# Up projection by seven Strassen block products on normed operands, down projection as its own stage

## The chip, the cores and the metric

The kernel runs on one core of a Trainium2 chip. A core has five engines with queues of their own: TensorE (PE, matrix products into PSUM; its weight loads are listed as PEld), VectorE (DVE), ScalarE (ACT), GpSimd (POOL) and SyncE (SP, which here only issues DMAs). The metric is the device time of one execution in microseconds (us), lower is better.

## The reference

One layer of a streaming encoder, for 1024 tokens of width 1024: a mixer (latent attention and a gated linear recurrence side by side, then an output projection with a residual), a feed-forward block, and a gated embedding. What matters here is the end:

```python
hf = rms_norm(x, g_ffn)
up = causal_dwconv(hf @ w_up, w_ffn_conv, b_ffn_conv)     # 1024 -> 2 * 2816, then 3 taps along the tokens
gte, val = up[..., :2816], up[..., 2816:]
x = x + (gelu(gte) * val) @ w_down                        # 2816 -> 1024
gate = sigmoid(rms_norm(x, g_ple) @ w_ple_gate + b_ple_gate)
x = x + gate * (p @ w_ple)
```

Everything is float32 at the interface. `rms_norm` divides by the root mean square over the 1024 channels and multiplies by a gain.

## The kernel before

Activations lie transposed: channels on the 128 partitions, tokens along the free axis. The residual x is eight channel tiles `x1[k][h]`, each in two halves h of 512 tokens. Every product is made of three matmuls, since each operand is split into a rounded high part and a rest, both in the fp32r type: high by high, high by low, low by high (`three`, L133). A split (`split`, L111) is an ACT cast for the high part and a DVE subtraction for the low part. With a gain, it is `scaled` (L116). `wload` (L121) brings a 128x1024 weight tile by DMA and splits it, in two-buffer tags `whi` and `wlo`. A matmul here has 128 rows, 128 output channels and 512 tokens, and is counted as one.

**Mix (L748 to L795).** For each half h, eight output channels c, each with two chains of 12 matmuls (`lru` and `at`), and four DVE operations on PSUM and x1 (L774, L775, L791, L792). After the loop of a half, `gained` (L837) makes from every x1 tile the split operand `h[k][h]` (ACT L118, DVE L119) and adds its square to a running sum (ACT L831, and L835 on DVE, or on POOL where `pool=True`). `measure` (L845, `stats` L139) sums the squares over partitions with eight small matmuls (L145) and takes the power -1/2 on POOL (L150). `scale` (L849, `spread` L153) spreads the result over partitions with two matmuls (L165), and ACT copies it to `r1` (L851).

**Feed-forward (L855 to L919).** 22 units j, each with a gate and a value block z of 128 channels. For each block PE runs 2 x 24 matmuls on the raw, gained operands, and the norm comes after the product: DVE multiplies the PSUM result by `r1` (L894). ACT makes the first tap with the bias (L896), DVE the other two (L898), ACT the gelu (L901), DVE the product of the two blocks (L902), which is split (L905). The down projection runs between the units, two units at a time (`GROUP`): 8 channels x 2 halves x 2 units x 3 matmuls, each PSUM result added to x1 by DVE (L873). The last two groups are done half by half, with `gained` for the gate's norm after each half (L914 to L918).

**Gate (`ple`, L940 to L969).** 16 chains of 24 matmuls, both halves of a channel in turn; the half's `measure` and `scale` come after the second and third chain for h = 0, after the fifth and sixth for h = 1. Four steps for each result: times r1 (L965), sigmoid (L966), times the embedding (L967), plus x1 (L968), and out by DMA. The embedding `e` was made during attention (`embed`, L921) and put in DRAM.

The order of each engine's instructions is the framework's: the order of the code is a priority, and an instruction whose inputs are late lets later ones go ahead. So the small matmuls of the gate's first `measure` stand in the trace at 1190.32 us, ahead of the gate's chains, which the code has first.

Of the kernel before, what the change touches and what calls it, by code (L numbers as in the profile page):

```python
# [19 lines left out]
P = 128  # L20
# [10 lines left out]
NL = 4  # L31
FF = 2816
NF = FF // P
GROUP = 2
# [41 lines left out]
class Block:  # L76
# [30 lines left out]
    def chain(self, out, terms, start=True, stop=True):  # L107
        for n, (w, x) in enumerate(terms):
            self.nc.tensor.matmul(out, lhsT=w, rhs=x, start=start and n == 0, stop=stop and n == len(terms) - 1)  # L109
# [104 lines left out]
    def project(self):  # L214
# [125 lines left out]
        self.ew.tile([P, 512], F32, name="pad1")  # L340
# [407 lines left out]
    def mix(self):  # L748
# [4 lines left out]
        self.r1 = x1p.tile([P, S], F32, name="r1")  # L753
        mx, ws, V = self.mx, self.wo, nc.vector
        self.mix_lru(1)
        self.h = [[None] * 2 for _ in range(NK)]
# [4 lines left out]
        for h in range(2):  # L761
# [8 lines left out]
            for c in range(NK + 2):  # L770
# [14 lines left out]
                if h == 1 and c == 4:  # L785
                    self.measure("x1", 0, D)
                if h == 1 and c == 5:
                    self.scale("x1", 0)
                if c >= 2:
                    o = at[c - 2]  # L790
                    V.tensor_tensor(out=o, in0=o, in1=self.r1[:, hs], op=ALU.mult)  # L791
                    V.tensor_tensor(out=self.x1[c - 2][h], in0=o, in1=self.x1[c - 2][h], op=ALU.add)  # L792
            self.gained(h, "g_ffn", "x1")
# [43 lines left out]
    def gained(self, h, gain, key, pool=False):  # L837

        nc = self.nc
        for k in range(NK):  # L840
            self.h[k][h] = self.pair(h)
            self.scaled(self.x1[k][h], self.col(gain, k), *self.h[k][h])
            self.square((key, h), k, self.x1[k][h], pool)
# [10 lines left out]

    def ffn(self):  # L855
        nc = self.nc
        V = nc.vector
        self.banks(sm=3, big=2)
        cf, fp = self.pool("ffn", 1, side="right")
        G, Wd = [], []  # L860

        def down(h, G, Wd, last=False):
            hs = slice(h * HALF, (h + 1) * HALF)
            for c in range(NK):
                if last and c % 3 == 1:
                    pair = self.acc("big")
                if last and c % 3:
                    ps = pair[:, (c % 3 - 1) * HALF:c % 3 * HALF]
                else:
                    ps = self.acc("sm")  # L870
                self.chain(ps, [q for a in range(len(G)) for q in self.three(
# [4 lines left out]
        for j in range(NF):  # L876
            br = []
            for z in range(2):
# [11 lines left out]
                if late and z == 0 and j < NF - 1:  # L890
                    for h in range(2):
                        down(h, *late)
# [162 lines left out]
```

## Time and profile before

| | us |
|---|---|
| median of 3 runs | 1287.68 (1286.81 to 1290.63) |
| profiled execution, device time | 1287.15 |
| its span, first to last instruction | 1285.4 |
| PE busy | 1253.8 (98%) |
| DVE busy | 864.4 (67%) |
| ACT busy | 525.6 (41%) |
| POOL busy | 166.0 (13%) |

The chain that ended last gives the stages: attention and what precedes it to about 369 us, mix to 462.6, the feed-forward block from there to 1190.3, the gate to the end. A busy time counts the union of an engine's instructions; a mean in nanoseconds is that of one instruction from start to end, which for PE and DVE overlaps the next one a little. "Idle" is the time for which the engine had nothing running ahead of an instruction, with what ended it.

### The profile page before, as it was taken

Reading aid. Unit: us, or ns where it says so; the run is one execution under the profiler, and the core shown is the slowest. Engines: PE = TensorE matmul, PEld = TensorE weight load, DVE = VectorE, ACT = ScalarE, POOL = GpSimd, SP = SyncE. Lnnn points to the kernel's source line nnn. Section 1 sums busy time; section 2 is a strip of 40 time slices with the busy share of each in tenths; the row PEclk is TensorE's granted clock in tenths of the full one; section 3 lists DMA queues with packets and bytes.
Section 4 is the critical chain, followed back from the end, with each engine's and each line's share of the span. In section 5 each row is a group of like instructions: output and inputs, shape, how many; then the busy total and the mean of one; then the engine's idle time right before and its main releaser. Section 6 shows DMA issues by size and latency. Waiting matters only on the chain.

```text
span 1285.4 us, 15152 instructions
## 1 busy us (share of the span) xinstructions
PE 1253.8 (98%) x5864; PEld 1047.6 (81%) x5864; DVE 864.4 (67%) x1266; ACT 525.6 (41%) x776; POOL 166.0 (13%) x180
## 2 busy tenths in 40 slices
PE   8998998999999999999999999999999999998998
PEld 6787986888878888888888888888888888886887
DVE  7789797778879777555656464646464646568464
ACT  7488678888863243212121212222222222225321
POOL 3013274444420000000000000000000000004200
PEclk9999998999999999999999999999999999998999
DMA  6213200111374110111111112111212021221141
GB/s 218 66 60 114 88 6 26 34 55 44 108 253 153 33 50 33 66 38 60 35 53 35 60 34 66 33 66 33 66 33 66 33 66 33 66 83 33 66 147 49
DMA packets 31351, 85.49 MB, mean 67 GB/s; under 512 B 3744, under 2 KB 6688, under 8 KB 31280
## 3 DMA queue, kind: packets, MB, share of 16 engines
q1 hardware_dynamic: 31280, 84.53, 20.0%
q8 instruction: 46, 0.75, 0.2%
q14 instruction: 25, 0.20, 0.1%
HBM read 69.84 MB, written 12.58 MB: 64 GB/s over the span
## 4 chain that ended last, share of the span: by engine, by line
PE 72%; DVE 2%; DMA 0%; issue 0%; POOL 0%; ACT 0%; POOLq 0%
PE big L109 39%; PE sm L109 16%; PE gt L109 7%; PE lru L109 4%; PE at L109 3%; DVE m L119 1%; PE p L736 0%; DVE x L873 0%; DMA om<-oc 0%; PE st L145 0%; PE p L717 0%; PE st L109 0%; PE st L165 0%; POOL at L744 0%; DVE u L898 0%
## 5 line engine op out<-in xcount | busy, mean ns | idle before, releaser
L109 PE MATMUL big<-m,whi 128*128 128x512 f32 x1408 | 433.7, 389 | 0.0
L109 PEld LDWEIGHTS big<-m,whi 128*128 128x128 f32 x1408 | 264.2, 188 | 54.8
L109 PE MATMUL big<-m,wlo 128*128 128x512 f32 x704 | 273.9, 389 | 0.0
L894 DVE TENSOR_TENSOR big<-big,r 128x1024 f32<-128x1024 f32 x44 | 54.2, 1232 | 189.8 <-PE big L109 189.8
L113 ACT CAST whi<-wraw 128x1024 fp32r<-128x1024 f32 (+2 forms) x68 | 67.9, 1002 | 248.6 <-PE big L109 208.9
L873 DVE TENSOR_TENSOR x<-sm,x 128x512 f32<-128x512 f32 x169 | 115.3, 689 | 63.2 <-PE sm L109 62.3
L109 PEld LDWEIGHTS big<-m,wlo 128*128 128x128 f32 x704 | 132.1, 188 | 27.5
L109 PE MATMUL sm<-gh,wh 128*128 128x512 f32 x316 | 123.2, 390 | 0.0
L109 PE MATMUL sm<-gl,wh 128*128 128x512 f32 x316 | 123.2, 390 | 0.0
L109 PE MATMUL sm<-gh,wl 128*128 128x512 f32 x316 | 123.2, 390 | 0.0
L898 DVE SCALAR_TENSOR_TENSOR u<-big,par,u 128x1023 f32<-128x1023 f32 x88 | 112.6, 1280 | 7.4 <-ACT u L896 6.0
L835 POOL TENSOR_TENSOR ssum<-ssum,sq 128x512 f32<-128x512 f32 x14 | 20.4, 1459 | 704.0 <-ACT sq L831 703.4
L114 DVE TENSOR_TENSOR wlo<-wraw,whi 128x1024 fp32r<-128x1024 f32 (+2 forms) x68 | 78.8, 1161 | 10.4 <-ACT whi L113 10.2
L109 PE MATMUL gt<-m,whi 128*128 128x512 f32 (+1 forms) x272 | 79.9, 377 | 0.0
L113 ACT CAST wh<-wraw 128x1024 fp32r<-128x1024 f32 x22 | 22.2, 1052 | 125.6 <-PE sm L109 119.8
L109 PE MATMUL big<-kT,qT 96*128 96x384 f32 (+11 forms) x288 | 68.7, 365 | 3.5 <-ACT kT L118 3.3
L109 PEld LDWEIGHTS sm<-gh,wh 128*128 128x128 f32 x316 | 59.6, 189 | 12.5
L109 PEld LDWEIGHTS sm<-gl,wh 128*128 128x128 f32 x316 | 59.5, 188 | 12.4
L109 PEld LDWEIGHTS sm<-gh,wl 128*128 128x128 f32 x316 | 59.5, 188 | 12.4
L896 ACT ACTIVATE u<-big,par 128x1024 f32<-128x1024 f32 x44 | 53.2, 1208 | 21.0 <-DVE big L894 21.0
L704 DVE TENSOR_SCALAR_CACHE_REDUCE pr<-big,nrq 128x512 f32<-128x512 f32 (+3 forms) x64 | 51.9, 814 | 11.7 <-PE p L717 4.3
L113 ACT CAST gh<-u 128x1024 fp32r<-128x1024 f32 x22 | 23.1, 1050 | 87.7 <-DVE u L902 87.7
(327 smaller groups left out, 2251.9 us busy)
## 6 DMA issues: line engine op xcount, KB each, us to landing
wraw<-w_up SPq DMA_DIRECT2D x44, 512.0 KB, 3.4
wraw<-w_down SPq DMA_DIRECT2D x22, 512.0 KB, 3.3
e<-eo SPq DMA_DIRECT2D x16, 256.0 KB, 2.0
m<-y SPq DMA_DIRECT2D x8, 512.0 KB, 6.8
x<-xT SPq DMA_DIRECT2D x16, 256.0 KB, 7.3
wraw<-w_gate SPq DMA_DIRECT2D x8, 512.0 KB, 3.4
e<-e SPq DMA_DIRECT2D x8, 512.0 KB, 3.5
out_dram<-gate SPq DMA_DIRECT2D x15, 256.0 KB, 2.1
```

What stands on the lines that cost most here:

```text
L109: self.nc.tensor.matmul(out, lhsT=w, rhs=x, start=start and n == 0, stop=stop and n == len(terms) - 1)
L113: self.nc.scalar.copy(hi, src)
L114: (self.nc.gpsimd if pool else self.nc.vector).tensor_tensor(out=lo, in0=src, in1=hi.bitcast(F32), op=ALU.subtract)
L119: self.nc.vector.scalar_tensor_tensor(out=lo, in0=src, scalar=gain, in1=hi.bitcast(F32), op0=ALU.mult, op1=ALU.subtract)
L704: V.tensor_scalar(out=pv, in0=sc, scalar1=self.nrq[:, qt, h:h + 1], scalar2=None, op0=ALU.mult, op1=ALU.min, accum_out=st[:, 0:1])
L835: (nc.gpsimd if pool else nc.vector).tensor_tensor(out=self.ssum[key], in0=self.ssum[key], in1=sq, op=ALU.add)
L873: V.tensor_tensor(out=self.x1[c][h], in0=ps, in1=self.x1[c][h], op=ALU.add)
L894: V.tensor_tensor(out=ps, in0=ps, in1=self.r1, op=ALU.mult)
L896: nc.scalar.activation(u, ps, AF.Identity, bias=self.col("cb", cj), scale=self.col("cw2", cj))
L898: V.scalar_tensor_tensor(out=u[:, d:], in0=ps[:, :S - d], scalar=self.col(f"cw{2 - d}", cj), in1=u[:, d:], op0=ALU.mult, op1=ALU.add)
```

## The change

The up projection is one level of Strassen's scheme in Winograd's form, for each unit. Its blocks are A (the weights): gate and value block by first and second half of the 1024 input channels; and B (the operands): first and second half of the channels by first and second half of the tokens. Seven products of 12 matmuls each (`product`) take the place of eight. The products accumulate in PSUM where the scheme allows it, and DVE and ACT make the remaining sums (`sums`).

- The operands have to be normed before they are added and subtracted, so DVE multiplies x1 by gain and `r1` in place (`normed`). x1 itself is first put in DRAM (`xs`), from where the down stage reads it.
- For tokens of half 0 the operands B11 and B21 are made during mix, from channel 4 of half 1 on; T1 to T4 and B22 at the start of the feed-forward stage, when `r1` of half 1 is there. The first two units share an order in which five products need half 0 alone.
- The weight blocks are added and split for each product, four products ahead (`weights`, `finish_weights`).
- The convolution, the gelu and the product of the two blocks are cut into five steps (`finish_unit`), one a product. The result is put in DRAM (`g`).
- The down projection is a stage of its own after all units: for each token half, eight PSUM banks accumulate over all 22 units; `w_down` and `g` are loaded and split in each half, two units ahead. `gained` for the gate's norm follows each half.
- `w_gate` is loaded and split during the second half of the down stage. The gate runs all of half 0 first, then half 1; `measure` and `scale` come after its first and second chain, and after the fourth and fifth.

After the lines of `ffn` that are shown come, in the code, T2, T3, T5 (which makes B22) and T4 for the four k each, with `run(5)` to `run(8)` and the weights 8 to 14 among them; `run(i)` is product i with its sums. The diff, cut to its core:

```diff
 # mix, in the loop over c of half h
+                    nc.sync.dma_start(out=self.xs[c - 2][:, hs], in_=x)
+                    self.square(("x1", h), c - 2, x)
+                if h == 1:
+                    if c == 2:
+                        self.measure("x1", 0, D)
+                        for z, u in ((0, 0), (1, 0), (0, 1)):
+                            self.fetch(u, z)
+                    if c == 3:
+                        self.scale("x1", 0)
+                    if 4 <= c < 8:
+                        for k in (c - 4, c):
+                            self.normed(k, 0)
+                            self.operand(("B21" if k >= NL else "B11", k % NL), self.x1[k][0], self.m[0])
+                            self.finish_operand()
+                        self.weights(c - 4)
+                        self.finish_weights(c - 4)
-            self.gained(h, "g_ffn", "x1")
...
+        self.order = [(0, 1), (0, 2), (1, 1), (1, 2), (2, 1)] + [(u, p) for p in (5, 6, 7, 3, 4) for u in range(2)]
+        for u in range(2, NF):
+            self.order += [(u, p) for p in (1, 5, 6, 2, 7, 3, 4) if (u, p) not in self.order]
...
+    def weights(self, i):                  # src is a block, or a sum of blocks made by DVE for p = 5, 6, 7, 3
...
+        self.nc.scalar.copy(t[:, :HALF], src)
...
+    def finish_weights(self, i):
...
+        self.nc.vector.tensor_tensor(out=lo, in0=src, in1=hi.bitcast(F32), op=ALU.subtract)
...
+    def product(self, i):
+        u, p = self.order[i]
+        b = {2: 1, 5: 3, 3: 3}.get(p, 2)
+        if p in (1, 2, 5):
+            self.bank[u, b] = self.acc(f"b{b}")
...
+        self.chain(self.bank[u, b], [q for k in range(NL) for q in self.three(
+            (hi, lo), self.B[x, k], (slice(None), slice(k * P, (k + 1) * P)), slice(None))],
+            start=p in (1, 2, 5), skip_group_check=True)
...
+    def sums(self, u, p):
+        if p == 1:
+            self.kept[u, 1] = self.keep(u, 2, self.ew, "ew", 3)      # keep: an ACT copy out of PSUM
+        elif p == 5:
+            self.kept[u, 5] = self.keep(u, 3, self.n, "sq", NTMP)
+        elif p == 6:
+            self.kept[u, 6] = self.keep(u, 2, self.n, "sq", NTMP)
+        elif p == 2:
+            V.tensor_tensor(out=self.out_tile(u, 0)[:, :HALF], in0=self.bank.pop((u, 1)), in1=self.kept.pop((u, 1)), op=ALU.add)
+        elif p == 7:
+            V.tensor_tensor(out=self.out_tile(u, 1)[:, HALF:], in0=self.bank[u, 2], in1=self.kept.pop((u, 5)), op=ALU.add)
+        elif p == 3:
+            V.tensor_tensor(out=self.out_tile(u, 0)[:, HALF:], in0=self.bank.pop((u, 3)), in1=self.kept.pop((u, 6)), op=ALU.add)
+        elif p == 4:
+            self.nc.scalar.copy(self.out_tile(u, 1)[:, :HALF], self.bank.pop((u, 2)))
+            self.epilogue += [(u, n) for n in range(5)]
...
+        if n < 2:                          # finish_unit; tap is the DVE operation that L898 was
+            t = self.u[u, n] = self.fp.tile([P, S], F32, tag=f"u{n}", name=f"u{n}", bufs=2)
+            nc.scalar.activation(t, self.U[u, n], AF.Identity, bias=self.col("cb", n * NF + u), scale=self.col("cw2", n * NF + u))
+        if n < 4:
+            tap(n // 2, n % 2 + 1)
+        if n == 3:
+            nc.scalar.activation(self.u[u, 0], self.u[u, 0], AF.Gelu_apprx_tanh)
+        if n == 4:
+            V.tensor_tensor(out=y, in0=self.u[u, 0], in1=y, op=ALU.mult)
+            nc.sync.dma_start(out=self.g[u], in_=y)
...
+        def T(n, k):                       # lo = x1[k], hi = x1[k + 4]; operand: ACT cast, then DVE subtraction
+            if n == 1:
+                self.normed(k, 1)
+                sub(lo[0], lo[1], lo[0])
+                self.operand(("T1", k), lo[0], m1)
+            elif n == 2:
+                self.normed(k + NL, 1)
+                self.finish_operand()
+                sub(lo[0], hi[1], lo[0])
+                self.operand(("T2", k), lo[0], m1)
+            elif n == 3:
+                sub(lo[1], hi[1], lo[1])
+                self.operand(("T3", k), lo[1], self.up, "B", 3 * NL)
+            elif n == 5:
+                self.operand(("B22", k), hi[1], self.up, "B", 3 * NL)
+            elif n == 4:
+                sub(hi[0], hi[0], lo[0])
+                self.operand(("T4", k), hi[0], self.up, "B", 3 * NL)
+        W, W2, M = self.weights, self.finish_weights, self.product
...
+        run(0)
+        W(4)
+        W(5)
+        self.measure("x1", 1, D)
+        W2(4)
+        W2(5)
+        run(1)
+        W(6)
+        W2(6)
+        self.scale("x1", 1)
+        W(7)
+        run(2)
+        run(3)
+        T(1, 0)
+        T(1, 1)
+        W2(7)
+        T(1, 2)
+        T(1, 3)
+        run(4)
...
+        for i in range(9, last + 1):
+            while n1 <= i + 4:
+                W(n1)
+                n1 += 1
+            while n2 <= i + 3:
+                W2(n2)
+                n2 += 1
+            M(i)
+            self.sums(u, p)
...
+            if self.epilogue and (p not in (2, 3) or len(self.epilogue) > 5):
+                self.finish_unit()
+            if i == last - 3:
+                self.start_down()          # loads of units 0 and 1
...
+    def load_down(self, n):
+        h, j = divmod(n, NF)
+        g = self.n.tile([P, HALF], F32, tag="sq", name="graw", bufs=NTMP)
+        self.nc.sync.dma_start(out=g, in_=self.g[j][:, h * HALF:(h + 1) * HALF])
+        self.dw[n] = self.wload(self.i["w_down"][j])
+        self.dg[n] = self.pair(1)
+        self.split(g, *self.dg[n])
+    def down(self):
+        for h in range(2):
+            ps = [self.acc("dn" if c < 7 else "st") for c in range(NK)]
+            for j in range(NF):
+                self.load_down(n + 2)
+                if j % 2 and j // 2 < NK:
+                    nc.sync.dma_start(out=self.x1[j // 2][h], in_=self.xs[j // 2][:, hs])
+                if h and j % 2 and j // 2 < NK:
+                    self.wg.append(self.wload(self.i["w_gate"][j // 2], gp, f"wg{j // 2}", 2))
+                for c in range(NK):
+                    self.chain(ps[c], self.three(w, g, (slice(None), slice(c * P, (c + 1) * P)), slice(None)), start=j == 0, stop=j == NF - 1, skip_group_check=True)
+                    if j == NF - 1:
+                        V.tensor_tensor(out=self.x1[c][h], in0=ps[c], in1=self.x1[c][h], op=ALU.add)
             for c in range(NK):
+                self.gained(c, h, "g_ple", "x2", pool=True)
...
-        for n, (_, h, c) in enumerate(sorted((c + h / 2, h, c) for c in range(NK) for h in range(2))):
+        for n, (h, c) in enumerate((h, c) for h in range(2) for c in range(NK)):
...
+            if n in (0, 3):
+                self.measure("x2", n // 3, D)
             if n in (1, 4):
-                self.measure("x2", n // 4, D)
-            if n in (2, 5):
-                self.scale("x2", n // 4)
+                self.scale("x2", n // 3)
```

More of the change, by code (lines that the diff above doesn't have):

```diff
@@ L33 @@
 NF = FF // P
-GROUP = 2
 NTMP = 4
@@ new lines, in fetch, with normed @@
+    def fetch(self, u, z):
+        if u >= NF:
+            return
+        if u % 2 and z:
+            r = self.up.tile([P, S], F32, tag="raw", name="raw", bufs=1)
+        else:
+            r = self.w.tile([P, S], F32, tag="wraw", name="wraw", bufs=3)
+        self.nc.sync.dma_start(out=r, in_=self.i["w_up"][2 * u + z])
+        self.raw[u, z] = r
+    def normed(self, k, h):
+        x = self.x1[k][h]
+        self.nc.vector.scalar_tensor_tensor(out=x, in0=x, scalar=self.col("g_ffn", k), in1=self.r1[:, h * HALF:(h + 1) * HALF],
+                                            op0=ALU.mult, op1=ALU.mult)
@@ L857, in ffn @@
         V = nc.vector
[L858 to L862, printed above, removed]
-            hs = slice(h * HALF, (h + 1) * HALF)
-            for c in range(NK):
[L865 to L871, printed above, removed]
-                    Wd[a], G[a], (slice(None), slice(c * P, (c + 1) * P)), (slice(None), hs))])
-                V.tensor_tensor(out=self.x1[c][h], in0=ps, in1=self.x1[c][h], op=ALU.add)
@@ L914, in ffn @@
-        down(0, *late, True)
-        down(0, G, Wd, True)
-        self.gained(0, "g_ple", "x2", pool=True)
-        down(1, late[0] + G, late[1] + Wd, True)
-        self.gained(1, "g_ple", "x2", pool=True)
-        self.c_ff, self.fp = cf, fp
+        self.banks(b1=2, b2=3, b3=2)
+        cu, self.up = self.pool("up", 1, side="right")
+        self.u = {}
+        x1, m1 = self.x1, self.m[1]
+        raw = self.up.tile([P, S], F32, tag="raw", name="raw", bufs=1)
+        nc.sync.dma_start(out=raw, in_=self.i["w_up"][3])
@@ new lines, in ffn @@
+        run(0)
[17 more added lines that the diff above has]
+        run(4)
+        W(8)
+        T(2, 0)
+        W2(8)
+        run(5)
+        T(2, 1)
+        T(2, 2)
+        run(6)
+        T(2, 3)
+        W(9)
+        T(3, 0)
+        W2(9)
@@ new lines, in ffn @@
+        W(10)
+        T(3, 1)
+        W2(10)
+        run(7)
+        T(3, 2)
+        T(3, 3)
+        W(11)
+        T(5, 0)
+        T(5, 1)
+        W2(11)
+        W(12)
+        T(5, 2)
+        T(5, 3)
+        W2(12)
+        run(8)
+        W(13)
+        W(14)
+        for k in range(NL):
+            T(4, k)
+        self.finish_operand()
+        W2(13)
+        W2(14)
+        self.close(self.c_x1)
+        cf, self.fp = self.pool("ffn", 1)
+        n1 = n2 = 15
+        last = len(self.order) - 1
```

186 lines of the change are left out of this document (125 added, 61 removed).

## The prediction

> **What bounds the kernel now.** I read the page first, then the chain of work that ended last, then busy time by stretch.
>
> ```profile
> PE 1253.8 (98%) x5864; PEld 1047.6 (81%) x5864; DVE 864.4 (67%) x1266; ACT 525.6 (41%) x776; POOL 166.0 (13%) x180
> ```
>
> ```profile
> 459.89 2.72 PE at L109 x12
> 462.61 5.44 PE big L109 x24
> 468.05 0.79 PE st L145 x8
> ...
> 474.44 0.45 PE st L165 x2
> ...
> 572.83 43.52 PE big L109 x192
> ...
> 1190.32 0.79 PE st L145 x8
> ```
>
> ```profile
> 462.60:1149.50 686.90, 686.90 (x3036) 568.87 (x3035) 398.73 (x409) 167.30 (x156) 1.01 (x1) 1.00 0.16 51
> 1149.50:1190.30 40.80, 36.09 (x147) 28.90 (x145) 37.16 (x42) 19.53 (x31) 17.01 (x12) 0.92 0.13 39
> ```
>
> The columns of the last view are: stretch, its length, busy time with instruction count of PE, PEld, DVE, ACT and POOL, granted clock, DMA share, GB/s. Through the whole feed-forward stage up to 1149.5 us PE has no gap: 686.90 busy of 686.90. DVE is at 58% there. So the time of this stage is a count of matmuls times their spacing. The spacing is 43.52/192 = 0.2267 us, or 2.72 us for a chain of 12. Only the stage's last 40.8 us have gaps, and a lower clock (0.92).
>
> **Up projection: matmuls removed.** Before: 44 blocks x 2 halves x 24 = 2112 matmuls, 478.7 us. After: 22 units x 7 products x 12 = 1848, 418.9 us. The difference is 264 x 0.2267 = **59.8 us**, all of it on PE's path. Down (1056 matmuls, 239.4 us) and gate (384) keep their counts.
>
> **The end of the feed-forward stage.** Before, 3168 matmuls and the two norms (0.79 + 0.45) should take 718.1 + 1.2 = 719.3 us. The stage takes 1190.3 - 462.6 = 727.7. So 8.4 us are lost, between 1149.5 and 1190.3: PE waits for the last unit's convolution and for DVE's sums.
>
> ```profile
> 1178.53 0.79 PE L109 MATMUL big<-gh,wh 128*128 128x512 f32 x1 [4.53 <-DVE x L873]
> 1179.12 0.63 PE L109 MATMUL big<-gl,wh 128*128 128x512 f32 x1
> 1179.55 0.63 PE L109 MATMUL big<-gh,wl 128*128 128x512 f32 x1
> ...
> 1184.67 0.42 PE L109 MATMUL sm<-gh,wh 128*128 128x512 f32 x1
> ```
>
> One gap of 4.53 us, and after it 14 matmuls at 0.43 us instead of 0.2267, until 1184.67: (1184.67 - 1178.53) - 14 x 0.2267 = 3.0 us more. In the new order the last unit's result is wanted 21 units later, and half 0's gate operands are ready 22 rounds ahead, so I let all 8.4 us go. What is late next there is the copy out of the last product's bank, which the down stage's accumulators take over; 0.5 us for that, up to 3 if ACT is behind.
>
> The floor is then 462.6 + 418.9 + 1.2 + 239.4 = 1122.1 at the gate's start. The gate has the same instructions and the same divided last chain; it runs from 1190.32 to the end, 95.1 us. Floor of the span: 1217.2 us.
>
> **DVE and ACT in a steady unit.** They must stay under PE's 7 x 2.72 = 19.04 us.
>
> ```profile
> L898 DVE SCALAR_TENSOR_TENSOR u<-big,par,u 128x1023 f32<-128x1023 f32 x44 | 56.4, 1281 | 6.2 <-ACT u L896 6.0
> L902 DVE TENSOR_TENSOR u<-u,u 128x1024 f32<-128x1024 f32 x22 | 27.0, 1225 | 0.7
> L835 DVE TENSOR_TENSOR ssum<-ssum,sq 128x512 f32<-128x512 f32 x20 | 13.7, 685 | 1.9 <-ACT sq L831 1.7
> L792 DVE TENSOR_TENSOR x<-at,x 128x512 f32<-128x512 f32 x16 | 10.9, 683 | 0.1
> L408 DVE SCALAR_TENSOR_TENSOR xc<-u,par,xc 128x1021 f32<-128x1021 f32 x4 | 5.1, 1283 | 0.1
> ```
>
> ```profile
> L896 ACT ACTIVATE u<-big,par 128x1024 f32<-128x1024 f32 x44 | 53.2, 1208 | 21.0 <-DVE big L894 21.0
> L901 ACT ACTIVATE u<-u 128x1024 f32<-128x1024 f32 x22 | 23.4, 1062 | 77.9 <-DVE u L898 77.9
> L113 ACT CAST ph<-p 128x512 fp32r<-128x512 f32 x34 | 19.5, 579 | 1.7 <-PE p L717 1.3
> ```
>
> DVE: four weight sums, seven subtractions and three sums out of PSUM, 14 x 0.685 = 9.6 us (L835 from SBUF and L792 from PSUM cost the same); four taps, now from SBUF, 4 x 1.28 = 5.1 (L408 shows that price from SBUF); the product 1.2. Sum 15.9 us, 84%. ACT: seven casts and four copies, 11 x 0.58 = 6.4; 2 x 1.21 + 1.06 = 3.5; sum 9.9 us. PE stays the bound, with weights prepared three to four products (8 to 11 us) ahead. I put the steady units at no loss; if DVE waits out 3 us in each, the cover is gone (a rival, below).
>
> **The start of the up stage** is where I expect the loss. Everything for half 1 hangs on `r1`, and PE has only five products until then.
>
> ```profile
> 415.51 1.40 DVE L119 SCALAR_TENSOR_TENSOR m<-x,par,m 128x512 fp32r<-128x512 f32 x2
> 416.83 0.69 DVE L791 TENSOR_TENSOR at<-at,r 128x512 f32<-128x512 f32 x1
> ...
> 449.20 0.68 DVE L835 TENSOR_TENSOR ssum<-ssum,sq 128x512 f32<-128x512 f32 x1
> 449.81 0.68 DVE L775 TENSOR_TENSOR x<-lru,x 128x512 f32<-128x512 f32 x1
> ```
>
> ```profile
> 475.22 0.57 ACT L851 COPY r<-st 128x512 f32<-128x512 f32 x1
> ```
>
> Back to back, DVE starts such an operation every 0.60 us (449.20 to 449.81), a scalar_tensor_tensor every 0.66 (two from 415.51 to 416.83). Before, `r1` of half 1 stood at 475.22 + 0.57 = 475.8. Its steps stay the same. DVE is fuller ahead of it: in half 1 of mix come eight norms, eight subtractions and four for the weights, 8 x 0.66 + 12 x 0.60 = 12.5 us, where before it had the like of gains. Against that the squares' sums come channel by channel and not at the end. I keep 475.8, with 4 us either way. From there T4 needs 8 norms (5.3 us), 16 subtractions (9.6), 20 low parts (12.0) and, interleaved, 13 weight operations (7.8): 34.7 us, so 510.5. PE unhindered wants T4 after 13 products: 462.6 + 13 x 2.72 + 1.2 = 499.2. **Loss 11.3 us**, range 4 to 18; the code makes the earlier operands in the same queue, so it falls mostly before the sixth product (T1) and in small pieces after. Matmuls in PE's queue wait behind it, DVE does not wait for PE, so a late PE adds nothing until T4 is there. Before T4, then, a slow clock after a gap (the 0.43 us above) costs nothing either; after the last gap it would cost at most those 3.0 us, and I take 0.
>
> By the Trainium skill, "TensorE: Matmul & The Clock Gate", part 1, an idle window of about 3.4 us halves PE's clock until some 3.4 us of work have passed; the 4.53 us gap agrees, with slow matmuls for 6.1 us. By that rule a last gap above its window adds up to the 3 us.
>
> **Spills.** Sixteen DMAs of x1 in mix and one of `g` a unit go to SP's queue, which waits at each for DVE; behind it stand the next weights. SP is idle for most of mix, and weights come one unit ahead.
>
> ```profile
> 395.39 0.33 SPq L124 DMA_DIRECT2D wraw<-w_down  x1
> 423.85 8.45 SPq L124 DMA_DIRECT2D wraw<-w_up  x2
> ```
>
> I take 0 for them, up to 2 us.
>
> **Down stage.** A round is 24 matmuls, 5.44 us.
>
> ```profile
> L113 ACT CAST wh<-wraw 128x1024 fp32r<-128x1024 f32 x22 | 22.2, 1052 | 125.6 <-PE sm L109 119.8 <-DMA wraw<-w_down 5.8
> L114 DVE TENSOR_TENSOR wl<-wraw,wh 128x1024 fp32r<-128x1024 f32 x22 | 26.0, 1218 | 1.6 <-ACT wh L113 1.6
> ```
>
> ```profile
> 375.00:421.70 46.70, 46.70 (x211) 38.78 (x210) 41.73 (x66) 19.58 (x31) 1.40 (x1) 1.00 0.51 184
> ```
>
> ACT needs 1.05 + 0.58 = 1.6 us, DVE 1.22 + 0.69 = 1.9, and the split has one round of 5.44 to be done in. DMA: 512 + 256 KB a round; at most, with x1 and `w_gate`, 2304 KB in two rounds, 217 GB/s. 184 GB/s took half of the DMA engines (0.51). So both hide. Where half 0 ends, `gained` stands in DVE's and ACT's queues ahead of the second split after it.
>
> ```profile
> L119 DVE SCALAR_TENSOR_TENSOR m<-x,par,m 128x512 fp32r<-128x512 f32 x32 | 30.2, 970 | 0.5 <-ACT m L118 0.4
> ```
>
> ```profile
> L119 DVE SCALAR_TENSOR_TENSOR m<-x,par,m x32: 736/745/1798, 412.3 to 1194.3; 128x512 fp32r<-128x512 f32 x32
> ```
>
> ```profile
> 1184.89 4.38 POOL L835 TENSOR_TENSOR ssum<-ssum,sq 128x512 f32<-128x512 f32 x3 [3.20 <-ACT sq L831]
> ```
>
> ```profile
> 1188.02 1.80 DVE L119 SCALAR_TENSOR_TENSOR m<-x,par,m 128x512 fp32r<-128x512 f32 x1
> ```
>
> The longest L119 (1.80 us, where the median is 0.745) ran beside POOL's sums. From the first finished channel, 7 x 3 x 0.2267 = 4.8 us ahead of the half's end, DVE has eight sums (8 x 0.60 = 4.8), eight low parts (6.0 at the median, 14.4 all slowed; 7.8 at the mean of 0.97, which I take since it comes from the same mixture) and one split (1.9): done 9.7 us after the end. The next split (1.9) ends 11.6 us after it, and PE wants it at 2 x 5.44 = 10.9. **Loss 1 us**, 0 to 7. The Trainium skill, "SBUF — State Buffer", "Who interferes with whom", has it that a DVE instruction with two SBUF inputs contends with a GpSimd instruction that reads SBUF. The row agrees; by the rule applied to all eight, the loss would be the 7.
>
> **Sum.** 1217.2 + 0.5 + 11.3 + 1 = 1230.0 us of span. Around the span lie 1287.15 - 1285.4 = 1.75 us, and the median is 0.5 above the profiled execution: **1232 us**, 56 less than before. Own range of this case 1223 to 1246.
>
> **Rivals.**
>
> 1. **The start is hidden.** The framework lets ready work go ahead, and a unit 2 product might fill the gap. For it: no DVE instruction before `r1` is short of inputs. Against: unit 2's next products need T1 too. Then the 11.3 us go: 1221.
> 2. **The feeders pace part of the units.** DVE at 84% is a mean; a product whose sum, subtraction and tap meet costs DVE 0.69 x 3 + 1.28 = 3.3 us against 2.72. For it: the steps of ACT and DVE alternate. Against: 3 to 4 products of stock. At 1 to 2 us a unit, 22 to 44 us: 1254 to 1276.
> 3. **Slower: a bank's hand-off.** Product 6 adds onto the bank of product 1, and must wait for ACT's copy of it; between them lies only product 5, 2.72 us. The same holds for 6 and 7, 7 and 4. If in ACT's queue a cast, the next Identity and a gelu that waits for two taps stand ahead of the copy, it ends 0.58 + 1.21 + 2 x 1.28 + 1.06 + 0.58 = 6.0 us after the product: PE waits 3.3 us. Once a unit that is 72 us: 1304. It decides from 56/22 = 2.5 us a unit. Against it: the code puts the copy ahead of the unit's own Identity and gelu.
> 4. **Down is late for its data.** With 184 GB/s as a ceiling, the eight pairs of rounds in half 1 (87 us) stretch by 217/184: 16 us more, 1248.
> 5. **The matmuls are not fewer.** The scheme needs three matmuls a term and 84 a unit in the diff; if four were needed, 112, 2464 in all, and 140 us more: 1372. I see nothing for it.
>
> **How the numbers follow.** Forecast 0.60, rival 1 0.12, rival 2 0.13, rival 4 0.06, rival 3 0.07, rival 5 or something that just eats the gain 0.02. The range runs from 1218 (rival 1 and 3 us of better luck) to 1256 (the forecast's end, rival 4, the lower edge of rival 2); outside stay rival 3 and most of rival 2. Faster by over 0.3% (about what a measurement of this kernel can tell from no change): 0.91, within it 0.02, slower 0.07.
>
> **What would show it.** After: 1848 up matmuls at 0.2267 us with PE without gaps from unit 2 on; idle time of PE between 470 and 510 us, ended by DVE low parts of T1 to T4, about 11 us in all; DVE near 84% in the steady stretch; no gap between the last product and the first down chain; one gap of about 1 us soon after half 0 of down; the gate 95 us from its first chain. I am wrong if PE's gaps repeat in every unit (rivals 2, 3), if they end on a DMA in down, or if mix itself becomes longer than 462.6 us.

## The result and the profile after

The median fell from 1288.65 us (4 runs, 1286.81 to 1290.63) to 1241.1 us (4 runs, 1239.53 to 1244.59): a ratio of 0.963, with a 95% interval from 0.961 to 0.966. The forecast was 1232 us, in a range from 1218 to 1256. The profiled execution of after has a device time of 1244.59 us, the slowest of the four, and a span of 1242.8 us, where the prediction's sum gave 1230.0; the spans of the other three are 1237.7 to 1240.2 us.

The head of the page of after, and its group of the up products:

```profile
span 1242.8 us, 15388 instructions
PE 1201.3 (97%) x5600; PEld 1001.7 (81%) x5600; DVE 896.6 (72%) x1406; ACT 643.6 (52%) x1030; POOL 165.8 (13%) x180
L108 PE MATMUL b<-B,A 128*128 128x512 f32 x1848 | 424.9, 392 | 3.7 <-DVE U L992 3.4
```

5600 matmuls instead of 5864: the 264 are gone, and PE is busy for 52.5 us less (1253.8 - 1201.3). The larger part of the 7.3 us between this and the 59.8 of the forecast, 4.4 us, are matmuls at a slow clock, which a busy time counts in full: below, 2.0, 2.7 and 2.7 us in after, against the 3.0 of before. Next, after by stretch, with the columns of the same view of before: start of the up stage, its steady part, down, gate.

```profile
464.30:512.20 47.90, 40.40 (x168) 32.23 (x166) 46.36 (x79) 23.20 (x41) 1.01 (x1) 0.92 0.16 52
530.00:890.00 360.00, 360.00 (x1590) 298.08 (x1589) 290.68 (x363) 182.57 (x265) 0.00 (x0) 1.00 0.24 85
898.60:1145.50 246.90, 241.97 (x1056) 199.84 (x1055) 111.80 (x120) 89.39 (x117) 12.05 (x8) 0.99 0.49 166
1145.50:1242.80 97.30, 90.90 (x429) 75.73 (x427) 47.38 (x70) 19.50 (x30) 11.42 (x8) 0.99 0.24 82
```

The steady part has PE busy for 360.00 of 360.00 us at full clock. At the start DVE is busy for 46.36 of 47.90 and PE for 40.40, the signature of a stage that DVE sets. In down and gate no engine but PE is near full, and PE still has 4.9 and 6.4 us of gaps. The list of PE's waits says where (engine, line, what it waited for: total, times, longest):

```profile
PE dn L108 <- DVE m L113: 4.9, 1, 4.9
PE st L144 <- DVE ssum L846: 3.8, 1, 3.8
PE b L108 <- DVE U L992: 3.4, 1, 3.4
PE st L164 <- DVE dg L162: 1.3, 1, 1.3
PE b L108 <- ACT keep L972: 0.3, 1, 0.3
```

Each occurs once, none is repeated by unit, and none ends on a DMA. The start in PE's order of time:

```profile
464.30 2.88 PE L108 MATMUL b<-B,A 128*128 128x512 f32 x12
470.98 1.87 PE L144 MATMUL st<-ones,ssum 128*128 128x1 f32 x8 [3.81 <-DVE ssum L846]
472.71 4.89 PE L108 MATMUL b<-B,A 128*128 128x512 f32 x12
...
497.57 11.24 PE L108 MATMUL b<-B,A 128*128 128x512 f32 x48 [0.32 <-ACT keep L972]
512.19 20.09 PE L108 MATMUL b<-B,A 128*128 128x512 f32 x76 [3.37 <-DVE U L992]
```

After the wait of 3.81 us twelve matmuls take 4.89 us, where the first twelve took 2.88. After the wait of 3.37 us, 76 matmuls take 20.09 us, and 76 x 0.2267 is 17.2: 2.7 us for the slow clock, the overlap of the last instruction (0.39 - 0.2267) taken off. The change of halves in down, first PE, then DVE, then POOL:

```profile
1028.96 0.61 PE L108 MATMUL dn<-m,whi 128*128 128x512 f32 x2
1034.51 0.80 PE L108 MATMUL dn<-m,whi 128*128 128x512 f32 x1 [4.93 <-DVE m L113]
1035.10 0.63 PE L108 MATMUL dn<-m,wlo 128*128 128x512 f32 x1
...
1040.11 0.62 PE L108 MATMUL dn<-m,whi 128*128 128x512 f32 x2
```

```profile
1019.45 1.62 DVE L113 TENSOR_TENSOR wlo<-wraw,whi 128x1024 fp32r<-128x1024 f32 x1
1021.00 10.58 DVE L118 SCALAR_TENSOR_TENSOR m<-x,par,m 128x512 fp32r<-128x512 f32 x8
1031.50 1.21 DVE L113 TENSOR_TENSOR wlo<-wraw,whi 128x1024 fp32r<-128x1024 f32 x1
1032.64 1.21 DVE L113 TENSOR_TENSOR wl<-wraw,wh 128x1024 fp32r<-128x1024 f32 x1
1033.77 1.88 DVE L113 TENSOR_TENSOR m<-graw,m 128x512 fp32r<-128x512 f32 x3
```

```profile
1020.59 8.45 POOL L846 TENSOR_TENSOR ssum<-ssum,sq 128x512 f32<-128x512 f32 x5 [0.60 <-ACT sq L842]
```

The third round of half 1 runs two matmuls that need only the high part of its operand `m`. From 1029.4 us on it wants the low part, and it gets that at 1034.46 (1033.77 + 0.69), behind eight low parts of 1.3 us on average (10.58 / 8) that run beside POOL's sums of squares. Thirteen matmuls at the slow clock, 1034.51 to 1040.11, add 5.60 - 13 x 0.2267 = 2.7 us to the gap of 4.93.

### The profile page after: what moved, and what is told of

Read it like the earlier page. It is cut to its first block, busy times and chain, and to the rows that moved or that the text cites. A ratio compares the mean times of both kernels' runs of the same rounds, so it can differ in the third digit from the quotient of the medians.

```text
span 1242.8 us, 15388 instructions
## 1 busy us (share of the span) xinstructions
PE 1201.3 (97%) x5600; PEld 1001.7 (81%) x5600; DVE 896.6 (72%) x1406; ACT 643.6 (52%) x1030; POOL 165.8 (13%) x180
## 4 chain that ended last, share of the span: by engine, by line
PE 66%; DVE 6%; issue 1%; DMA 0%; ACT 0%; POOL 0%; POOLq 0%; DVEq 0%
PE b L108 31%; PE dn L108 16%; PE gt L108 6%; PE lru L108 4%; PE at L108 3%; PE st L108 2%; DVE m L118 1%; DVE B L911 1%; PE big L108 1%; DVE x L1038 1%; DVE x L1177 1%; DVE x L896 0%; PE p L734 0%; PE st L144 0%; DMA om<-oc 0%
## 5 line engine op out<-in xcount | busy, mean ns | idle before, releaser
L108 PE MATMUL b<-B,A 128*128 128x512 f32 x1848 | 424.9, 392 | 3.7 <-DVE U L992 3.4
L108 PEld LDWEIGHTS b<-B,A 128*128 128x128 f32 x1848 | 349.7, 190 | 78.0 <-issue 3.8
L108 PE MATMUL dn<-m,whi 128*128 128x512 f32 x616 | 191.9, 392 | 4.9 <-DVE m L113 4.9
L108 PEld LDWEIGHTS dn<-m,whi 128*128 128x128 f32 x616 | 116.8, 190 | 29.9 <-DVE m L113 5.4
L108 PE MATMUL dn<-m,wlo 128*128 128x512 f32 x308 | 120.9, 392 | 0.0
L1004 DVE SCALAR_TENSOR_TENSOR u<-U,par,u 128x1023 f32<-128x1023 f32 x88 | 112.4, 1278 | 2.1 <-ACT u L1009 2.0
L944 ACT CAST A<-s 128x512 fp32r<-128x512 f32 x88 | 54.7, 622 | 78.0 <-PE b L108 70.8
L108 PE MATMUL gt<-m,wh 128*128 128x512 f32 (+1 forms) x272 | 80.0, 377 | 0.0
L952 DVE TENSOR_TENSOR A<-s,A 128x512 fp32r<-128x512 f32 x88 | 60.6, 689 | 14.7 <-ACT A L944 14.6
L108 PEld LDWEIGHTS dn<-m,wlo 128*128 128x128 f32 x308 | 58.5, 190 | 12.1
L972 ACT COPY keep<-b 128x512 f32<-128x512 f32 x66 | 38.4, 583 | 52.4 <-PE b L108 52.4
```

Source lines behind the costliest of these rows:

```text
L944: self.nc.scalar.copy(t[:, :HALF], src)
L952: self.nc.vector.tensor_tensor(out=lo, in0=src, in1=hi.bitcast(F32), op=ALU.subtract)
L972: self.nc.scalar.copy(t, self.bank[u, b])
L1004: tap = lambda z, d: V.scalar_tensor_tensor(out=self.u[u, z][:, d:], in0=self.U[u, z][:, :S - d], scalar=self.col(f"cw{2 - d}", z * NF + u ...
```

## The experiments

Every run is a change to the kernel after. Times in us; a ratio is to the kernel before on the same chip, with its 95% interval. The stage lengths are those of one profiled execution: up from the first matmul of `b` to the first of `dn`, down from there to the first of `gt`, gate from there to the end.

| | median | ratio | up starts | up | down | gate |
|---|---|---|---|---|---|---|
| after (first run) | 1241.1 | 0.963 [0.961, 0.966] | 464.3 | 435.2 | 246.0 | 97.3 |
| e1_after_again | 1243.13 | 0.9662 [0.9647, 0.9677] | 463.2 | 435.0 | 246.0 | 97.4 |
| e2_spread | 1232.69 | 0.9583 [0.9569, 0.9598] | 460.9 | 433.9 | 238.2 | 97.1 |
| e3_dve_plus2 | 1241.96 | 0.9657 [0.9643, 0.9672] | 462.3 | 433.9 | 246.0 | 97.1 |
| e4_dve_plus4 | 1243.52 | 0.9660 [0.9644, 0.9676] | 463.2 | 435.4 | 247.3 | 97.1 |
| e5_eight | 1297.70 | 1.0076 [1.0061, 1.0091] | 469.2 | 484.8 | 244.9 | 97.4 |
| e6_start_plus8 | 1247.10 | 0.9688 [0.9670, 0.9706] | 461.6 | 438.4 | 245.4 | 97.1 |
| e7_start_pool | 1248.37 | 0.9694 [0.9678, 0.9710] | 464.0 | 439.7 | 245.8 | 97.4 |
| e8_fill | 1240.38 | 0.9637 [0.9623, 0.9652] | 463.6 | 432.3 | 245.0 | 97.3 |
| e9_half_dve | 1235.32 | 0.9600 [0.9586, 0.9614] | 461.8 | 433.9 | 240.0 | 97.0 |
| e10_dve_plus12 | 1287.48 | 1.0008 [0.9998, 1.0017] | 462.8 | 478.6 | 246.4 | 97.1 |
| e11_best | 1233.52 | 0.9585 [0.9571, 0.9599] | 463.6 | 434.3 | 238.2 | 95.2 |
| e12_gate_late | 1239.79 | 0.9632 [0.9615, 0.9648] | 462.8 | 433.9 | 245.9 | 95.3 |

The up stage starts between 460.9 and 464.3 us in executions whose code up to there does the same (all but e5). The stage itself takes 435.2 and 435.0 us in after and e1, and 433.9 in e2, e9 and e12, with the same code in it. So a total moves by some 4 us for nothing. An edit worth 2 us is read from the length of its stage, and at the start of the up stage from the time at which product 4, the first that needs T4, begins.

**e1_after_again**: the kernel after, unchanged.

> The changed kernel once more, as a second profile of it. If the losses found in its first profile belong to the kernel, they stand again at the same places: the wait of about 3.4 us at the start of the up stage that a DVE sum ends, and 4.9 us where half 0 of down ends; the median comes out near 1241 us. If the slow matmuls after such a gap depend on how the gap falls against the clock's own measure, the count of slow matmuls after each gap (about 14 at 0.43 us) changes from one profile to the next, and with it the span, by 1 to 3 us.

The same three waits (4.9, 3.8, 3.4 us) and stage lengths within 0.2 us: the waits belong to the order of the work, not to one execution. What a wait costs in slow matmuls behind it is another matter, as further executions show. These are the 1692 matmuls from product 4 to the end of the up stage, without a gap, in after, e1 and e2:

```profile
512.19 386.38 PE b L108 x1692
510.93 386.32 PE b L108 x1692
508.43 385.37 PE b L108 x1692
```

At 43.52/192 us each they need 383.5 us, and 0.16 us of each row is the end of the last instruction. So one gap of 3.4 us costs 2.7 and 2.6 us in two executions and 1.7 in the third. Why it is the one or the other, no run here shows. For all runs but e5, whose edits follow, in us:

| | product 4 begins, from the stage's start | gap ahead of it | lost in slow matmuls behind it |
|---|---|---|---|
| after | 47.9 | 3.37 | 2.7 |
| e1 | 47.7 | 3.41 | 2.6 |
| e2, e3, e9, e10, e12 | 47.5 | 3.40 to 3.44 | 1.7 |
| e4 | 48.4 | 3.42 | 1.5 |
| e6 | 52.4 | 3.69 | 1.4 |
| e7 | 55.0 | 1.70 | 0.1 |
| e8 | 47.5 | 0.70 | 0.1 |
| e11 | 49.5 | 2.04 | 0.1 |

**e2_spread**: half 0's `gained` for the gate is not done at the change of halves, but one channel in every second round of half 1.

```diff
+                if h and j % 2 == 0 and 0 < j <= 2 * NK:
+                    self.gained(j // 2 - 1, 0, "g_ple", "x2", pool=True)
...
-            for c in range(NK):
+            for c in range(NK if h else 0):
                 self.gained(c, h, "g_ple", "x2", pool=True)
```

> The eight gained steps of token half 0 are no longer in one block at the end of half 0 of down, but one in every second round of half 1. Theory A (DVE's and ACT's queue is full of them, so the split of a later round's operands is late): the 4.9 us gap of PE goes, and with it the slow clock behind it (14 matmuls, 2.9 us): 7 to 8 us less than the changed kernel, about 1233 us. Rival B (the data come late from DRAM there, since spilled results, down weights, gate weights and x1 all load at once): the loads stay where they are, the gap stays, 1241 us.

Down fell from 246.0 to 238.2 us (it is 245.0 to 246.0 in e1, e6, e8 and e12, whose down stage has no edit, so 7 to 8 us are the edit's), the wait of 4.9 us is gone from the list, and the loads are the same as before the edit. So the gap and the slow clock behind it came from these instructions in the queues, and neither from late data nor from the change of halves as such. Another 2.3 us of the total are an earlier start of the up stage, and 1.1 a cheaper gap within it; the edit touches neither.

**e9_half_dve**: half 0's squares are summed on DVE instead of POOL, at the same place.

```diff
-                self.gained(c, h, "g_ple", "x2", pool=True)
+                self.gained(c, h, "g_ple", "x2", pool=h == 1)
```

> The squares of token half 0 at the end of its down stage are summed on DVE instead of POOL, the order stays. Theory A1 (the gap of 4.9 us is the length of DVE's queue, whoever makes it long): DVE has 7 x 0.60 = 4.2 us more sums, its eight gained steps take 0.66 instead of about 1.3 us, 5 us less: the gap stays within 1.5 us of 4.9, the total at 1240 to 1244 us. Rival (what makes the queue late is POOL reading beside DVE, and the square tiles that POOL frees slowly): the gap falls by 3 us or more, and with it the slow clock, 1236 us.

DVE has seven operations more at the change, and yet down is 6.0 us shorter than in e1 (240.0). The DVE and PE rows of e9 there:

```profile
1018.66 0.75 DVE L118 SCALAR_TENSOR_TENSOR m<-x,par,m 128x512 fp32r<-128x512 f32 x1
```

```profile
1026.70 1.89 PE L108 MATMUL dn<-m,whi 128*128 128x512 f32 x7 [1.43 <-ACT m L112]
```

Each of the eight low parts takes 0.75 us, and the gap is 1.43 us, ended by ACT. So most of the 4.9 us is due to POOL's part in the work, not to the number of DVE's instructions. The loads of `g` share the square tiles (tag `sq`) that POOL frees, and could have been late for that. But in after ACT had cast the high part of the late operand by 1027.4 us, and DVE has no idle time from 1013.5 us until the low part is done at 1034.46. So what held the operand there is the length of DVE's queue, with its slower operations, and not a late load.

**e3_dve_plus2, e4_dve_plus4, e10_dve_plus12**: in every unit past the third, 4, 8 or 12 of the low parts of the weights are computed once more, so many DVE operations more.

```diff
+        for _ in range(1 + (i > 20) * (2 if p in (1, 5, 6, 7, 3) else 1)):      # e10
             self.nc.vector.tensor_tensor(out=lo, in0=src, in1=hi.bitcast(F32), op=ALU.subtract)
```

> Four of the seven low-part subtractions of a unit are done twice, from unit 2 or 3 on: 4 x 0.60 = 2.4 us more of DVE in each unit. In the changed kernel DVE is busy for 290.7 of 360 us in the steady stretch, 15.4 us of a unit's 19.04, so 3.7 us are free. Theory (PE is the bound, DVE has cover): no change, 1241 us within noise, DVE at 93% of the steady stretch. Rival (the hand-offs are already tight, PE waits a little for DVE as soon as it is later): 20 units x 2.4 = up to 48 us more.

> All seven low-part subtractions of a unit are done twice, one of them three times: 8 x 0.60 = 4.8 us more of DVE in each unit, 20.2 us against PE's 19.04. Theory (DVE throughput decides, from 3.7 us on): every unit is 20.2 us long, 20 units x 1.2 = 23 us more, about 1264 us, with PE gaps in every unit that DVE ends. If the stock of prepared products were no help, it would be 20 x 4.8 = 96 us more.

> All seven low parts of a unit are done twice and five of them three times: 12 x 0.60 = 7.2 us more of DVE in each unit. Back to back DVE needs (14 x 0.60 + 4 x 1.2 + 1.14) = 14.3 us a unit in the changed kernel, now 21.5 against PE's 19.04. Theory (DVE's throughput decides from 4.7 us a unit on, and its price is the back-to-back spacing and not the mean duration): about 20 units x 2.5 = 50 us more, 1290 us, no faster than the kernel before. If it stayed below 1255, something else than throughput sets the units.

The steady part, 530 to 890 us, of e3, e4 and e10:

```profile
530.00:890.00 360.00, 360.00 (x1590) 298.10 (x1589) 334.92 (x438) 184.31 (x267) 0.00 (x0) 1.00 0.24 85
```

```profile
530.00:890.00 360.00, 360.00 (x1590) 298.20 (x1589) 359.37 (x507) 180.72 (x266) 0.00 (x0) 1.00 0.23 82
```

```profile
530.00:890.00 360.00, 340.13 (x1423) 260.46 (x1422) 360.00 (x519) 158.04 (x236) 0.00 (x0) 1.00 0.20 72
```

In e3 DVE is at 93%, as expected, and nothing changes. In e4 DVE is busy for 359.37 of 360 us, and PE has no gap: no loss in the up stage, where one was expected (down is 1.3 us longer, with a second wait for DVE). In e10 DVE is full, and PE does 1423 matmuls where it did 1590. Its waits for low parts now recur (total, times, longest):

```profile
PE b L108 <- DVE A L954: 16.2, 33, 0.7
```

The reason is the price. An operation of 0.685 us lets the next begin after 0.60. By this spacing the steady unit costs DVE 14 x 0.60 + 4 x 1.20 + 1.1 = 14.3 us. With 8 more it is 19.1, against PE's 19.04: exactly full. With 12 more it is 21.5, and 19 units lose 2.5 us each, 47; measured 43.6 (478.6 - 435.0). So the break point lies between 8 and 12 more operations, as the spacing has it; the change's margin was about 4.7 us a unit, and in e10, beyond it, the whole gain is eaten.

**e5_eight**: everything of the new structure (normed operands, spills, down as its own stage), but eight plain products a unit: no sums of blocks, no `keep`, no T.

```diff
-            self.order += [(u, p) for p in (1, 5, 6, 2, 7, 3, 4) if (u, p) not in self.order]
+            self.order += [(u, z, t, k) for z in range(2) for k in range(2) for t in range(2)]
```

> Undoes Strassen alone: eight products of 12 matmuls a unit instead of seven, each weight block split once and used for both token halves, no sums of blocks; everything else as in the changed kernel (normed operands made in mix, spilled results, down as a stage, gate by halves). Theory (the gain of the change is the matmuls that it saves): 22 x 12 x 0.2267 = 59.8 us more in the up stage; its start needs 8 norms and 8 low parts after r1, 10.1 us of DVE instead of some 32, so most of the 14 us of loss there goes, say 9: about 1241 + 60 - 9 = 1292 us, 2 to 8 us above the kernel before. Rival (a good part of the gain comes from the new stages, which remove the waits at the end of the feed-forward block): clearly below the kernel before, 1275 us or less.

1297.7 us: 10 us more than the kernel before, and 54.6 more than e1 (53 by the ratios). The rest of the rebuild alone is thus a loss, and the gain is the matmuls'. The 10.9 us of span (1296.3 - 1285.4) are made up so: the up stage begins 6.6 us later than in before (469.2 against 462.6; 4.2 of them a wait of PE just ahead of it), takes 484.8 where 2112 matmuls and the norms need 480.0, down and gate are 5.5 and 2.3 over 239.4 and 95.1, and the 8.4 us at the old stage's end come off: 6.6 + 4.8 + 5.5 + 2.3 - 8.4 = 10.8. The time is 5.7 us above the 1292 that was expected. Some 4 of these lie at the start: the wait and the up stage lose 9.0 us (4.2 + 4.8), where about 5 of after's 14 were to remain.

```profile
PE b L108 <- ACT sq L842: 4.2, 1, 4.2
```

**e6_start_plus8**: the eight low parts of T2 and T3 are computed twice, 4.8 us of DVE.

```diff
+            for _ in range(2 if key[0] in ("T2", "T3") else 1):
                 self.nc.vector.tensor_tensor(out=lo, in0=src, in1=hi.bitcast(F32), op=ALU.subtract)
```

> Eight low-part subtractions of T2 and T3 are done twice at the start of the up stage: 8 x 0.60 = 4.8 us more of DVE between r1 and T4. Theory (DVE's throughput from r1 to T4 sets when product 4 can run): the wait before it grows from 3.4 to about 8 us, 4.8 us more in all, 1246 to 1248 us. Rival (the start is a chain of hand-offs between DVE, ACT and PE, with DVE waiting in it): no change, or less than 2 us.

Product 4 begins 52.4 us after the stage's start, 4.6 us later than in e1 and 4.8 later than in e2, e9 and e12. The wait just ahead of it is 3.7 us and not 8: the rest of the waiting came earlier, before matmuls that needed a low part. The up stage is only 3.4 us longer than in e1, and the ratio 0.0026, or 3.3 us, higher, since this gap cost 1.4 us in slow matmuls and that of e1 2.6. So DVE's work between `r1` and T4 sets the start, about one us for each us.

**e7_start_pool**: the sums and low parts of the weights 8 to 14 go to POOL, ten of their operations from 477.5 us on.

```diff
-        V = self.nc.vector
+        V = self.nc.gpsimd if 8 <= i <= 14 else self.nc.vector
...
+        (self.nc.gpsimd if 8 <= i <= 14 else self.nc.vector).tensor_tensor(out=lo, in0=src, in1=hi.bitcast(F32), op=ALU.subtract)
```

> At the start of the up stage the sums and low parts of the weights for products 8 to 14 (11 to 13 operations) run on POOL instead of DVE. Theory (DVE throughput): DVE saves up to 13 x 0.60 = 7.8 us before T4, so the wait before product 4 goes and the span falls by 5 to 7 us, about 1235 us. Rival (DVE and POOL contend for reads where DVE reads two SBUF operands, as the slow steps beside POOL's sums show, 1.80 us for 0.745): DVE's own operations grow beside POOL's some 19 us of work, by about as much as was saved; 1241 us or worse.

The up stage got longer, by 4.7 us. Product 4 begins 7.3 us later than in e1, but behind a gap of 1.70 us and so without slow matmuls. DVE and POOL in e7:

```profile
483.98 0.68 DVE L911 TENSOR_TENSOR B<-x,B 128x512 fp32r<-128x512 f32 x1
484.58 1.78 DVE L896 SCALAR_TENSOR_TENSOR x<-x,par,r 128x512 f32<-128x512 f32 x1
486.29 1.77 DVE L911 TENSOR_TENSOR B<-x,B 128x512 fp32r<-128x512 f32 x1
487.98 1.77 DVE L1038 TENSOR_TENSOR x<-x,x 128x512 f32<-128x512 f32 x1
489.68 0.74 DVE L896 SCALAR_TENSOR_TENSOR x<-x,par,r 128x512 f32<-128x512 f32 x1
```

```profile
483.53 3.98 POOL L952 TENSOR_TENSOR A<-s,A 128x512 fp32r<-128x512 f32 x2 [4.42 <-ACT A L944]
487.59 1.62 POOL L938 TENSOR_TENSOR s<-wraw,s 128x512 f32<-128x512 f32 x1
```

For as long as POOL works, each DVE operation takes 1.77 us instead of 0.68, and when POOL stops it is back at 0.74. Each operation that DVE does beside POOL costs it 1.1 us more, which is more than the 0.6 us that one moved operation saves it. This is the rule of the Trainium skill, "SBUF — State Buffer", "Who interferes with whom", that a DVE instruction with two SBUF inputs contends with a GpSimd one that reads SBUF; the trace agrees, with a factor of 2.6.

**e8_fill**: fourteen matmuls whose result is not used stand in PE's queue before the product that waits for T4, into a free bank.

```diff
+            if i == 13:
+                ps = self.acc("st")
+                for n in range(14):
+                    nc.tensor.matmul(ps, lhsT=self.ones_r, rhs=self.B["T1", 0][0], start=True, stop=True)
             M(i)
```

> Fourteen matmuls of no use (3.2 us at the fast spacing), into the bank of the norms, stand in PE's queue where it waits 3.4 us for the first product that needs T4. Theory (the slow matmuls behind that gap come from the idle clock): the gap closes, the 14 matmuls after it take 0.2267 us instead of 0.43, 2 to 3 us less than the changed kernel, in the up stage alone. Rival (the slowness behind the gap is contention or DVE pacing): no change, or some tenths more.

The gap shrinks to 0.70 us and the matmuls after it run at full clock, 21.13 us for 92, or 0.230 each:

```profile
507.51 2.88 PE L1123 MATMUL st<-B,ones_r 128*128 128x512 f32 x12
511.09 21.13 PE L108 MATMUL b<-B,A 128*128 128x512 f32 x92 [0.70 <-DVE U L992]
```

Twelve of the fourteen stand in the gap. With work added, the up stage is 2.7 us shorter than in e1, and 1.6 shorter than in e2, e9 and e12, where the same gap cost less. Product 4 begins no earlier (47.5 us). So the 1.6 to 2.7 us are the clock's, and not the gap's. The ratio is lower by 0.0025, with intervals that just overlap.

**e12_gate_late**: half 0's `measure` and `scale` in the gate come one chain later.

```diff
-            if n in (0, 3):
+            if n in (1, 3):
                 self.measure("x2", n // 3, D)
-            if n in (1, 4):
+            if n in (2, 4):
                 self.scale("x2", n // 3)
```

> Only the gate's measure and scale of half 0 come one chain later. Theory (the two spreading matmuls stand in PE's queue 1.3 us before DVE, which is still in gained of half 1, has made their operand): the gate stage falls from 97.3 to about 95.5 us, 1.3 to 2 us in all. Rival (the 2 us are lost elsewhere, in the last chains and the way out): no change.

The gate takes 95.3 us instead of 97.4, and the wait of 1.3 us before the gate's spreading matmuls (L164) is gone. For that line 0.4 us are still listed, which belong to the start of the up stage.

**e11_best**: e2, e8 and e12 together, and half 1's `measure` after the second product instead of before it, against the wait of 3.81 us.

> Four edits of the changed kernel together: the gained steps of half 0 spread over half 1 of down (-7.8 us in the down stage by the second run here), fourteen matmuls of no use where PE waits for T4 (-2.7), the first norm's small matmuls after the second product instead of the first (PE waited 3.8 us for them, r1 perhaps 1 us earlier), and the gate's norm of half 0 one chain later (-1.5 to -2 in the gate stage, by its 97.3 us against 95.1 before). Sum: 12 to 14 us less than the changed kernel, 1228 to 1230 us. Rival for the start: since DVE and not PE sets it, filling and moving PE's matmuls there gives nothing: 1231 to 1233.

Down and gate gave what they gave alone (238.2 and 95.2), the start nothing (434.3, where e2 has 433.9), so the time is that of the rival and not the 1228 to 1230 of the sum. PE's rows in e11:

```profile
476.96 0.47 PE L164 MATMUL st<-dg,ones_r 128*128 128x512 f32 x1 [3.52 <-DVE dg L162]
...
492.58 0.39 PE L1123 MATMUL st<-B,ones_r 128*128 128x512 f32 x1
...
513.14 7.05 PE L108 MATMUL b<-B,A 128*128 128x512 f32 x30 [2.04 <-DVE U L992]
```

The wait moved to the spreading matmuls. `r1` stood 15.3 us after the stage's start (14.3 in e2): 1 us later, and not earlier as expected. DVE waited 0.9 us for it, and then 0.7 for casts of ACT. Eight of the unused matmuls were scattered by the framework from 492.58 us on, where there was no gap. Six stood ahead of product 4; its gap shrank to 2.04 us and cost nothing in slow matmuls, but it began 49.5 us after the stage's start, 2.0 us later than in e2. That took what the clock gave. In total e11 does not differ from e2 (0.9585 and 0.9583). These two have the lowest ratios to before, 0.958, where after itself has 0.963 to 0.966.

## Why the prediction was right, and where its terms were off

The time was 9 us over the forecast, inside its range. Stage by stage, against the sum of 1230.0, with the profiled 1242.8 (some 3 us of the 12.8 between them belong to this execution, the slowest of the four):

| term | predicted | measured | difference |
|---|---|---|---|
| mix ends | 462.6 | 464.3 | +1.7 |
| up, 1848 matmuls and norms | 420.1 | 420.1 | 0 |
| start of up: lost ahead of product 4 | 11.3 | 11.3 | 0 |
| start of up: clock behind the last gap | 0 | 2.8 | +2.8 |
| last product to down | 0.5 | 0 | -0.5 |
| down: change of halves | 1 | 7.6 | +6.6 |
| gate | 95.1 | 97.3 | +2.2 |

The start is measured so: 13 products, 156 matmuls, stand before 512.19, and 464.3 + 156 x 0.2267 + 1.2 = 500.9, so 11.3 us are lost ahead of it; from 512.19 the chain runs 386.38 us without a gap, 2.8 more than 1692 x 0.2267. A longer mix was named as a sign of being wrong. Over the twelve executions with the same code it ends between 460.9 and 464.3 us, with the 462.6 of before near the middle, so nothing shows that it became longer.

**Matmuls removed: right.** PE has no gap in the steady part, and e5 shows that the count is what the gain comes from: with eight products the new structure is 0.8% slower than the old.

**Steady unit: right in what bounds it, wrong in a price.** DVE was put at 15.9 us a unit (84%); the trace has 81%, or 15.4. But I added up durations, 0.69 us, and took what remained to 19.04 as the room. e4 shows that busy share is not yet need: at 99.8% nothing is lost, since an operation's end overlaps the next. By the spacing of 0.60 the need is 14.3 us. I used that spacing for the start and not here, and for e4 it made me expect a loss that isn't there.

**Start of the up stage: right in what bounds it, hit in size partly by luck, wrong in where PE waits.** `r1` stood at 478.9, 14.6 us after the stage's start where the sum had 13.2 (475.8 - 462.6). T4 stood at 510.8; the 31.9 us between them are 2.8 under the 34.7 of the sum, since eight weight operations stand there in DVE's queue and not thirteen. And the product does not start with T4 but behind a sum out of its bank (L992) 1.4 us later, in the same DVE queue. The three errors, +1.4, -2.8 and +1.4, cancel, and that is luck.

```profile
510.16 0.68 DVE L911 TENSOR_TENSOR B<-x,B 128x512 fp32r<-128x512 f32 x1
510.76 0.68 DVE L952 TENSOR_TENSOR A<-raw,A 128x512 fp32r<-128x512 f32 x1
511.36 1.28 DVE L992 TENSOR_TENSOR U<-b,keep 128x512 f32<-128x512 f32 x2
```

That the start is DVE's is shown by e6. But the prediction put most of the loss ahead of the sixth product, as waits for T1, and no wait of PE ends on T1. PE lost 3.81 us earlier, to the last sum of squares of half 1, 3.37 ahead of product 4 and 0.32 between. Another 3.1 us are slow matmuls behind the first wait (2.0 in twelve of a product, 1.1 in the eight small ones, 1.87 against 0.79 in before). The prediction also let a slow clock ahead of T4 cost nothing, since DVE does not wait for PE. That holds only in part: the matmuls that spread `r1` stand behind the second product in PE's queue. Where that product took 5.47 us (e4), product 4 began 48.4 us after the stage's start, and where it took 4.48 (e12), 47.5.

**Clock behind the last gap: mis-sized.** I gave it 0, "at most those 3.0 us". The gap was 3.37 us and cost 2.7 here, and 1.5 to 2.7 over eight executions with a gap of 3.37 to 3.44; e8 took nearly all of it away. The Trainium skill, "TensorE: Matmul & The Clock Gate", part 1, puts the window at about 3.4 us; this gap lay at that edge, and the clock fell in all eight. I named the rule and did not work out from my own loss that a last gap of that size was likely.

**Change of halves: mis-sized, 1 against 7.6.** Two errors. The low parts were priced at 0.97 us, the mean of a mixture. Here their median is 1.78 and eight take 10.5 us instead of 7.8 (one row, min/median/max in ns):

```profile
L118 DVE SCALAR_TENSOR_TENSOR m<-x,par,m x8: 739/1776/1785, 1021.0 to 1030.8; 128x512 fp32r<-128x512 f32 x8
```

And DVE's queue held two weight splits that the sum left out, one for a round ahead and one of `w_gate`, 1.5 and 1.1 us (and one low part of `g` less, 0.7). The operand came 16.2 us after the end of half 0 (1018.3, from 898.6 + 528 x 0.2267) instead of 11.6. A gap of 4.93 then brought the slow clock, 2.7 us, which the term did not have. Nearest was the 7 that the rule of the Trainium skill, "SBUF — State Buffer", "Who interferes with whom", gave; the trace agrees, with five of the eight slowed (5 x 1.7 + 3 x 0.66 = 10.5). That the 7 comes so near the 7.6 is luck, since it held neither the two splits nor the slow clock. e2 and e9 show the place and POOL's part in it.

**Gate: a step left out.** I took it over at 95.1. But `measure` and `scale` come one chain earlier than before, and the spreading matmuls wait for DVE; e12 gives the 2 us back.

**Spills, and loads of down: right.** No wait of PE ends on a DMA, at 166 GB/s over the down stage. ACT waits seven times for `g` there, 12.9 us in all, and PE for none of it.

**Rivals.** 1 (start hidden) is excluded by the waits, 3 and 4 by the lack of any wait by unit or on a DMA, 5 by the count of 1848. Rival 2 did not happen; e10 shows that it exists. With 8 more operations a unit (19.1 us of DVE) PE loses nothing yet, with 12 more (21.5 us) the whole gain.

## What to carry to other kernels

Where a matrix engine without gaps sets the time, fewer matmuls are worth their spacing, and what has to be worked out is whether the engines that feed it keep up: by the spacing of their instructions back to back, not by their durations, and in the transitions more than in the steady part. A gap of 3.4 us or more on PE cost another 1.4 to 2.7 us here in slow matmuls, so late work is better spread over the rounds than put at the seam of two stages. Work that is moved to POOL to relieve DVE can slow down every DVE operation beside it.

## What the runs showed of the hardware

- DVE operations with two SBUF inputs, 128x512, take 1.77 us beside a POOL operation that reads SBUF, and 0.68 to 0.75 without it (e7, e9).
- DVE at 99.8% busy (e4) still left PE without a gap in the steady part: durations of 0.685 us overlap, and 0.60 us is the need.
- A gap of PE of 3.37 to 3.69 us cost 1.4 to 2.7 us in slow matmuls behind it, in nine executions, and one of 4.9 us 1.7 to 2.7 us, in ten; the same gap costs more in one execution than in another. Gaps of 0.70 to 2.04 us cost 0.1 (e7, e8, e11). Twelve unused matmuls in the gap kept the clock (e8).
- Identical code up to the up stage reaches it between 460.9 and 464.3 us.
